# Two hybrid backbone layers on one core: where the residual is scaled, and in which order the up-projection's operands are made

## The chip, the cores and the metric

One core of one Trainium2 chip runs the whole program. The metric is the device time of one execution in microseconds (us), taken as the median of several runs.

The engines are named as in the profile. PE is TensorE, and PEld is its weight load. DVE is VectorE, ACT is ScalarE and POOL is GpSimd. SP is the engine from whose queue most transfers are issued. Some transfers are issued from POOL's queue; here these are the ones that add to what lies at the destination (`accum_op=ALU.add`).

## What is computed

The reference runs two layers over 1024 latent tokens and 256 context tokens, 1024 channels wide. Each layer mixes tokens (attention, a gated recurrence, a Fourier mix, one output projection) and then runs a gated feed-forward network with a width-3 convolution. What matters here is the end of each sub-layer:

```python
x1 = layer_norm(ALPHA * x + g1 * mix, ln1_g[l], ln1_b[l])
ffn = conv_ffn(x1 * (1 + sc2) + sh2, w_up[l], conv_w[l], conv_b[l], w_down[l])
x = layer_norm(ALPHA * x1 + g2 * ffn, ln2_g[l], ln2_b[l])

def conv_ffn(h, w_up, conv_w, conv_b, w_down):
    u = h @ w_up
    up = jnp.pad(u, ((0, 0), (1, 1), (0, 0)))
    u = up[:, :-2] * conv_w[0] + up[:, 1:-1] * conv_w[1] + up[:, 2:] * conv_w[2] + conv_b
    a, g = jnp.split(u, 2, axis=-1)
    return (a * jax.nn.silu(g)) @ w_down
```

So `ALPHA * x1`, the residual of the second update, is the normalised row times `ALPHA * ln1_g` plus `ALPHA * ln1_b`. All values are fp32. Layer 0 treats both streams, layer 1 only the latent one.

## The kernel before

**Matmuls.** A product of two fp32 operands is made from three passes: each operand is split into a high part, rounded by ACT, and a low part, the difference, made by DVE or POOL (`mm3`, lines 156 to 161). A "split" below is that pair of instructions.

**Order on the engines.** The program is written as one stream. A scheduler then places the instructions of each engine, by its own estimate of when each becomes ready, so the order on an engine need not be the order of the text. Each engine and each issuing queue then works strictly in its own order. Tiles of one tag share `bufs` buffers; a new tile waits until the readers of the old one are done.

**Output projection** (`out_tile`, line 1037). Ten tiles of 128 tokens in layer 0, eight in layer 1, in stages that overlap. A tile loads its residual (`resid_in`), multiplies with `w_out` (16 accumulations of three matmuls), adds and normalises (`normalise`), stores the normalised row to `y1[i]` (line 1071) and then stores its transpose to `yT` (`put_T`). In layer 1 the residual is multiplied by a row `ga` on POOL (line 1009), and a row `ba`, prepared by a load, a multiply on ACT and a store (lines 1700 to 1704), is added by an accumulating transfer (line 1010). While the last tiles run, `later_half` (line 1165) makes the operands B11 and B21 from the later 512 tokens, its low parts on POOL.

**Up-projection.** The 2816 pairs of columns are 22 blocks `j`. For each block the four quarter-products of a 2x2 scheme are made from seven smaller ones, listed in `ORDER` (line 1202): a weight operand (A11, A12, A22 or a sum S1 to S4) times a data operand (B11, B21, B22 or a combination T1 to T4), each 12 matmuls of 512 columns. For the first six blocks (`EARLY`) the two products with B11 and B21 need only the later tokens. `up_early` (line 1192) makes them ahead and parks them in DRAM, two blocks inside the output projection's stage and four after it.

`combined_halves` (line 1171) makes the other five data operands. It goes through the four quarters `k` of the channels: it loads and modulates the four raw pieces of a quarter, makes T1 to T4 of that quarter, and splits all five operands of that quarter; T1 and T4 get their low parts on POOL. It is called between the last four `up_early`.

`up_all` (line 1239) then goes through blocks 0 to 21. A block writes into two tiles U of 128x1026 (value and gate). For an early block the parked product comes back by a transfer into U's later half (lines 1269 and 1289); the first product is added to it, and the third accumulates onto the first one's PSUM bank. `gate(j)` runs the convolution on each half of both tiles (two DVE instructions each, line 1120), the gating, and one store per half. `up_weights` sums and splits each weight operand by itself, 128x512 at a time (lines 1219 and 1231 to 1233).

**Down-projection** (`down_all`, line 1403). The same scheme: seven products P1, P7, P6, P4, P5, P3, P2 in that order, each in six steps over 11 blocks. Weight and activation operands are put together in place by accumulating transfers from POOL's queue (`plus`, line 1344). The residual of a tile comes in `load_r`, which `PLAN` (line 1466) ties to a product and a step: the four later tiles in P6 steps 2 to 5, the four earlier ones where `DOWN_AT` says.

```python
nc.scalar.copy(r[:, 0:1], after)                # load_resid, lines 992 to 999: after = a value of this step
nc.sync.dma_start(out=r, in_=src)
e0.tensor_tensor(out=r, in0=r, in1=ga, op=ALU.mult)   # DVE in down_all, POOL in ffn_down
e1.tensor_tensor(out=r, in0=r, in1=ba, op=ALU.add)
```

In layer 0 the context tokens' feed-forward follows (`ffn_up`, `ffn_down`, line 1511); there the two instructions on `r` stand on POOL, two tiles.

Of the kernel before, what the change touches and what calls it, by code (L numbers as in the profile page):

```python
# [19 lines left out]
P = 128  # L20
D = 1024
# [34 lines left out]
DOWN_AT = ((("P34", "P35", "P23", "P24"), ("P21", "P22", "P24", "P25"), ("P21", "P22", "P24", "P25"), ("P21", "P22", "P23", "P24")),  # L56
           (("P34", "P35", "P21", "P22"), ("P21", "P22", "P23", "P24"), ("P21", "P22", "P23", "P24"), ("P34", "P35", "P20", "P21")))
# [39 lines left out]
def hybrid_backbone_kernel(ctx: ExitStack, tc: tile.TileContext, A: dict, out: bass.AP):  # L97
# [890 lines left out]
    def load_resid(pp, src, ga, ba, bufs=4, after=None, engs=None):  # L988
        r = pp.tile([P, D], F32, tag="r", bufs=bufs, name="r")
        if after is not None:  # L990

            nc.scalar.copy(r[:, 0:1], after)
        nc.sync.dma_start(out=r, in_=src)
        if ga is None:
            nc.scalar.mul(r, r, ALPHA)
        else:
            e0, e1 = engs or (nc.gpsimd, nc.gpsimd)
            e0.tensor_tensor(out=r, in0=r, in1=ga, op=ALU.mult)
            e1.tensor_tensor(out=r, in0=r, in1=ba, op=ALU.add)
        return r  # L1000

    def resid_in(src, late):
        pp, _, ga, ba = late
# [33 lines left out]
    def out_tile(l, i, S, pa, late, wo, src, y1, yT):  # L1037
# [22 lines left out]
        pp, g1 = late[0:2]  # L1060
# [86 lines left out]
    def h_pair(hp, nm):  # L1147
        return tuple(hp.tile([P, 4, HALF], F32R, name=nm + x) for x in "hl")

    def load_quarter(rp, yT, t0, k, cols, tag, bufs, eng=None):  # L1150
        r = rp.tile([P, HALF], F32, tag=tag, bufs=bufs, name="hraw")
        nc.sync.dma_start(out=r, in_=yT[k * P:(k + 1) * P, CTX + t0:CTX + t0 + HALF])
        a, b = (c[:, k:k + 1] for c in cols)
# [6 lines left out]
    def split_to(pair, k, src, eng):  # L1160
        hi, lo = (t[:, k, :] for t in pair)
# [9 lines left out]
    def combined_halves(h, rp, yT, cols):  # L1171
        for k in range(4):
            b11, b21, b12, b22 = (load_quarter(rp, yT, t0, kk, cols, f"raw{t0}{kk // 4}", 1 if t0 else 2, e)
                                  for t0, kk, e in ((HALF, k, nc.scalar), (HALF, k + 4, nc.scalar), (0, k, None), (0, k + 4, None)))
            yield
            t1, t2, t3, t4 = (rp.tile([P, HALF], F32, tag=f"t{x}", bufs=1, name="hcomb") for x in range(4))
            for o, x, y in ((t1, b12, b11), (t2, b22, t1), (t3, b22, b12), (t4, t2, b21)):
                nc.vector.tensor_tensor(out=o, in0=x, in1=y, op=ALU.subtract)
            yield
            for nm, src, eng in (("T2", t2, nc.vector), ("T1", t1, nc.gpsimd), ("T3", t3, nc.vector), ("T4", t4, nc.gpsimd),  # L1180
                                 ("B22", b22, nc.vector)):
                split_to(h[nm], k, src, eng)
            yield

    def up_product(w, b, bank, onto=None):
        acc = psu([P, HALF], "pu", bank) if onto is None else onto
        for k in range(4):
            mm3(acc, tuple(t[:, k, :] for t in w), tuple(t[:, k, :] for t in b), k == 0 and onto is None, k == 3,
# [13 lines left out]
    ORDER = (("A11", "B11"), ("A12", "B21"), ("S2", "T2"), ("S1", "T1"), ("S3", "T3"), ("A22", "T4"), ("S4", "B22"))  # L1202

    def up_weights(l, fp):
# [8 lines left out]
        def operand(j, nm):  # L1213
            if nm[0] == "A":
                return quarter(j, nm)
            if (j, nm) not in made:
                for o, x, y, op in (("S1", "A21", "A22", ALU.add), ("S2", "S1", "A11", ALU.subtract),
                                    ("S3", "A11", "A21", ALU.subtract), ("S4", "A12", "S2", ALU.subtract)):
                    t = fp.tile([P, 4, P], F32, tag=o, bufs=1, name=o)
# [4 lines left out]
        def splits(todo):  # L1224
            for n, (j, nm) in enumerate(todo):
                if n % 2 == 0:
                    own = n // 2 % 5 > 2
# [635 lines left out]
```

## Time and profile before

| | us |
|---|---|
| median of 3 runs | 3336.25 (3333.35 to 3342.41) |
| the profiled execution's own time | 3349.57 |
| its span in the profile | 3347.8 |
| PE busy, share of the span | 3098.0 (93%) |
| DVE busy | 2363.9 (71%) |
| ACT busy | 1585.6 (47%) |
| POOL busy | 772.6 (23%) |

The profiled execution is 13.3 us longer than the median. A busy PE is not PE at its peak: the granted clock (PEclk, 1.00 is 2.4 GHz, 0.50 is 1.2 GHz) says at what rate it ran. In the span, layer 0's output projection ends and `up_early` runs until 926.8; its up-projection runs from 946.3 to about 1395, its down-projection to 1640, the context tokens' part to about 1860. Layer 1's up-projection runs from 2665.7 to about 3083, its down-projection to 3322.

### The profile page before, as it was taken

The page shows a single profiled execution, that of the slowest core. Times are in us where ns is not written, and L with a number is a line of the kernel's source. Part 1 is how long each engine was busy: PE and PEld are TensorE (multiplying, and loading weights), DVE is VectorE, ACT ScalarE, POOL GpSimd, SP SyncE. Part 2 cuts the span into 40 slices and gives each one's busy share as a digit, 9 for nine tenths or more (in the row PEclk, how much of TensorE's full clock was granted, in tenths as well). Part 3 has the DMA queues.
Part 4 walks back from the last instruction along what each step waited for, and adds up shares of the span by engine and source line. Part 5 has one row for each costly group of instructions (what it writes and reads, how often), then busy time and mean ns, then how long its engine had stood idle before and what let it go on. Part 6 is the DMA issues. An engine that isn't in the chain of part 4 may idle for free.

```text
span 3347.8 us, 55191 instructions
## 1 busy us (share of the span) xinstructions
PE 3098.0 (93%) x20897; PEld 2526.6 (75%) x20897; DVE 2363.9 (71%) x4377; ACT 1585.6 (47%) x3169; POOL 772.6 (23%) x820
## 2 busy tenths in 40 slices
PE   6999998999979999999999999998978789999996
PEld 4878977787756777677797788876767677887785
DVE  4623567887687877668876754668777778887678
ACT  3324556674444544434454435655652434554332
POOL 3522114432210000021245351115425300000222
PEclk9999999999989999999999999998889899999998
DMA  7652232107655444597775432122028632223973
GB/s 216 201 159 80 59 98 58 39 15 237 212 186 158 129 130 131 162 252 197 235 211 173 133 106 71 47 85 73 21 82 228 207 110 85 85 76 116 277 185 126
DMA packets 450255, 456.51 MB, mean 136 GB/s; under 512 B 31859, under 2 KB 343620, under 8 KB 449990
## 3 DMA queue, kind: packets, MB, share of 16 engines
q1 hardware_dynamic: 420006, 404.53, 38.4%
q0 software_dynamic: 29984, 48.46, 7.7%
q8 instruction: 164, 2.69, 0.3%
q14 instruction: 101, 0.83, 0.1%
HBM read 358.36 MB, written 94.55 MB: 135 GB/s over the span
## 4 chain that ended last, share of the span: by engine, by line
PE 47%; DVE 11%; DMA 5%; POOL 3%; issue 2%; ACT 2%; SPq 1%; POOLq 0%; DVEq 0%; ACTq 0%
PE pu L159 9%; PE pu L160 8%; PE pu L161 8%; PE pd L159 3%; PE pd L160 3%; PE pd L161 3%; PE ps_t L603 2%; PE ps_s L567 1%; PE ps_o L613 1%; DMA araw<-act 1%; DVE cv L1120 1%; DVE wlo L1387 1%; PE ps_s L568 1%; PE pws L159 1%; PE ps_o L615 1%
## 5 line engine op out<-in xcount | busy, mean ns | idle before, releaser
L570 DVE TENSOR_REDUCE mx<-ps_s 128x1 f32<-128x512 f32 (+1 forms) x400 | 222.4, 588 | 109.7 <-PE ps_s L568 108.6
L1345 POOL DMA_DIRECT2D X<-in_w_down_dram x48 | 55.4, 1154 | 1028.9 <-DMA X<-in_w_down_dram 945.1
L609 DVE TENSOR_TENSOR pl<-ps_t,ph 128x512 fp32r<-128x512 f32 x328 | 223.0, 686 | 88.1 <-ACT ph L608 86.1
L603 PE MATMUL ps_t<-ident,p 128*128 128x128 f32 x1312 | 265.5, 286 | 14.2 <-DVE pl L609 8.7
L608 ACT CAST ph<-ps_t 128x512 fp32r<-128x512 f32 x328 | 191.0, 589 | 162.8 <-PE ps_o L615 81.7
L577 ACT ACTIVATE p<-ps_s,mx 128x512 f32<-128x512 f32 (+1 forms) x400 | 243.2, 617 | 52.2 <-DVE mx L573 42.4
L160 PE MATMUL pd<-wlo,whi 128*128 128x512 f32 x616 | 248.4, 403 | 14.0 <-DVE wlo L1387 12.3
L159 PE MATMUL pd<-whi,wlo 128*128 128x512 f32 x616 | 242.8, 401 | 16.9 <-DVE wlo L1387 12.7
L1120 DVE SCALAR_TENSOR_TENSOR cv<-U,cw,cv 128x512 f32<-128x512 f32 x352 | 247.1, 748 | 12.9 <-ACT cv L1117 12.8
L161 PE MATMUL pd<-whi 128*128 128x512 f32 x616 | 247.7, 402 | 0.0
L159 PE MATMUL pxs<-whi,hlo 128*128 128x256 f32 x752 | 221.5, 295 | 5.8 <-DVE hraw L1566 4.3
L145 POOL TENSOR_TENSOR wlo<-raw,whi 128x1024 fp32r<-128x1024 f32 x63 | 152.5, 2423 | 281.0 <-ACT whi L144 281.0
L160 PE MATMUL pxs<-wlo,hhi 128*128 128x256 f32 x752 | 216.5, 288 | 0.6 <-DVE wlo L145 0.4
L161 PE MATMUL pxs<-whi,hhi 128*128 128x256 f32 x752 | 216.2, 288 | 0.0
L613 PE MATMUL ps_o<-pl,V 128*128 128x256 f32 x656 | 202.8, 326 | 6.6 <-DVE pl L609 4.0
L603 PEld LDWEIGHTS ps_t<-ident,p 128*128 128x128 f32 x1312 | 166.2, 144 | 38.2 <-DVE pl L609 14.7
L1117 ACT ACTIVATE cv<-U,cb,cw 128x512 f32<-128x512 f32 x176 | 138.1, 815 | 111.4 <-DVE U L1248 99.3
L615 PE MATMUL ps_o<-ph,V 128*128 128x256 f32 x656 | 184.7, 299 | 0.0
L1232 ACT CAST whi<-S 128x512 fp32r<-128x512 f32 x176 | 106.4, 620 | 149.2 <-PE pu L161 113.3
L144 ACT CAST whi<-raw 128x1024 fp32r<-128x1024 f32 x130 | 136.0, 1049 | 84.3 <-DMA raw<-in_w_up_dram 30.7
L567 PE MATMUL ps_s<-KT,qt 128*128 128x512 f32 (+1 forms) x400 | 150.8, 408 | 6.4 <-ACT p L577 3.0
L159 PEld LDWEIGHTS pxs<-whi,hlo 128*128 128x128 f32 x752 | 143.5, 191 | 15.3 <-issue 7.4
(401 smaller groups left out, 9160.4 us busy)
## 6 DMA issues: line engine op xcount, KB each, us to landing
raw<-in_w_up_dram SPq DMA_DIRECT2D x144, 512.0 KB
raw<-in_w_ada_dram SPq DMA_DIRECT2D x96, 512.0 KB
raw<-in_w_down_dram SPq DMA_DIRECT2D x52, 512.0 KB
act<-cv SPq DMA_DIRECT2D x88, 256.0 KB
X<-in_w_down_dram POOLq DMA_DIRECT2D x40, 512.0 KB, 9.6
raw<-in_w_in_dram SPq DMA_DIRECT2D x36, 512.0 KB
y<-r SPq DMA_DIRECT2D x28, 512.0 KB
araw<-act SPq DMA_DIRECT2D x26, 512.0 KB
```

What stands on the lines that cost most here:

```text
L159: nc.tensor.matmul(o, lhsT=al, rhs=bh, start=start, stop=False, skip_group_check=onto)
L160: nc.tensor.matmul(o, lhsT=ah, rhs=bl, start=False, stop=False, skip_group_check=onto)
L161: nc.tensor.matmul(o, lhsT=ah, rhs=bh, start=False, stop=stop, skip_group_check=onto)
L567: nc.tensor.matmul(t[:, 0:n], lhsT=qt[:, h % (2 * QT_PAIRS), :], rhs=KT[:, 2 * kv + 1, s0:s0 + n], start=True, stop=False)
L570: nc.vector.tensor_reduce(out=mx[:, j:j + 1], in_=t[:, 0:n], axis=AX.X, op=ALU.max)
L577: nc.scalar.activation(out=t, in_=sc[j][:, 0:n], func=AF.Exp, bias=mx[:, 3:4], accum_out=su[:, h, j:j + 1])
L603: nc.tensor.transpose(t[:, ss, h, :], in_=ps2[h][2 * s2 + ss], identity=ident)
L608: nc.scalar.copy(ph, tv)
L609: nc.vector.tensor_tensor(out=pl, in0=tv, in1=f32(ph), op=ALU.subtract)
L613: nc.tensor.matmul(o, lhsT=V[:, s, kv, 1:3, :].rearrange("p a c -> p (a c)"), rhs=pl[:, ss, :], start=(s == 0), stop=False)
L615: nc.tensor.matmul(o, lhsT=V[:, s, kv, 0:2, :].rearrange("p a c -> p (a c)"), rhs=ph[:, ss, :], start=False, stop=(s == nk - 1))
L1120: nc.vector.scalar_tensor_tensor(out=o, in0=u[:, tap:tap + n], scalar=convw[l][tap][:, c:c + 1], in1=o, op0=ALU.mult, op1=ALU.add)
```

## The change

1. `out_tile` stores `y1` later: after `put_T` the row is multiplied by a new row `gn` = `ALPHA * ln1_g` on POOL, then stored. A new DRAM row `bn` = `ALPHA * ln1_b` is made by `scaled_row` (load, ACT multiply, store).
2. `load_resid` fills `r` with `bn`, broadcast by a transfer from SP, and adds `y1` by an accumulating transfer from POOL. The two multiplying and adding instructions are gone, as are the loads of the rows `ga` and `ba` in `rows`. The tag `r` has 8 buffers instead of 6; the earlier tiles' loads are in P5, steps 2 to 5.
3. `combined_halves` goes operand by operand: all B11 and B21 pieces, then T2 for all quarters, then T1, T3, B22, T4. All low parts are on DVE. Its tiles reuse each other's places.
4. Six weight operands are split ahead (`ready_w`) between the steps of 3. Blocks 6 and 7 go first, then 0 to 5, then the rest. In `ORDER` S4 comes before A22. Two operands that lie side by side are split by one pair of 128x1024 instructions.
5. `gate` works on 1024 columns at once, value first, and stores once.

```diff
-DOWN_AT = ((("P34", "P35", "P23", "P24"), ("P21", "P22", "P24", "P25"), ...
-           (("P34", "P35", "P21", "P22"), ("P21", "P22", "P23", "P24"), ...
+DOWN_AT = ((("P52", "P53", "P54", "P55"), ("P21", "P22", "P24", "P25"), ...
+           (("P52", "P53", "P54", "P55"), ("P21", "P22", "P23", "P24"), ...
...
+    def load_resid(pp, src, b, after):
+        r = pp.tile([P, D], F32, tag="r", bufs=8, name="r")
+        nc.scalar.copy(r[:, 0:1], after)
+        nc.sync.dma_start(out=r, in_=b.partition_broadcast(P))
+        nc.gpsimd.dma_start(out=r, in_=src, accum_op=ALU.add)
         return r
 
+    def scaled_row(pp, src, nm):
+        t = pp.tile([KD, P], F32, tag="brow", bufs=1, name="brow")
+        nc.sync.dma_start(out=t, in_=src.rearrange("(k p) -> k p", p=P))
+        nc.scalar.mul(t, t, ALPHA)
+        o = scratch(nm, [D])
+        nc.sync.dma_start(out=o.rearrange("(k p) -> k p", p=P), in_=t)
+        return o
...
         normalise(pp, r)
-        nc.sync.dma_start(out=y1[i], in_=r)
         tag = yield
         put_T(r, yT, i * P, pp, tag=tag or "u")
+        nc.gpsimd.tensor_tensor(out=r, in0=r, in1=gn, op=ALU.mult)
+        nc.sync.dma_start(out=y1[i], in_=r)
...
+        for k in range(4):
+            b11.append(fetch("B11", place("T3h", k), k, nc.scalar))
+            b21.append(fetch("B21", place("B22l", k), k, nc.scalar))
             yield
+        for k in range(4):
+            b12.append(fetch("B12", place("B22h", k), k, nc.scalar))
+            b22.append(fetch("B22", place("raw2", k), k))
+            t1.append(sub(place("T3l", k), b12[k], b11[k]))
+            t2.append(sub(place("raw1", k), b22[k], t1[k]))
+            split_into("T2", k, t2[k])
             yield
+        for k in range(4):
+            split_into("T1", k, t1[k])
+            yield
+        for k in range(4):
+            split_into("T3", k, sub(place("T4h", k), b22[k], b12[k]))
+            yield
+        t4 = [sub(t2[k], t2[k], b21[k]) for k in range(4)]
+        for k in range(4):
+            split_into("B22", k, b22[k])
+            yield
+        for k in range(4):
+            split_into("T4", k, t4[k])
             yield
...
-    ORDER = (..., ("S3", "T3"), ("A22", "T4"), ("S4", "B22"))
+    ORDER = (..., ("S3", "T3"), ("S4", "B22"), ("A22", "T4"))
...
+                if nm == "A22":
+                    hl, n = [fp.tile([P, 512], F32R, tag=t + "y", bufs=2, name=t) for t in ("whi", "wlo")], 4
+                    src = operand(j, nm)
+                else:
+                    todo.pop(0)
+                    own = wide % 4 == 3
+                    wide += 1
+                    hl = [(fp if own else wp).tile([P, 1024], F32R, tag=t + "x" * own, bufs=1 if own else 3, name=t)
+                          for t in ("whi", "wlo")]
+                    n = KD
...
-        todo = [(j,) + o for j in range(NJ) for o in ORDER if ...]
+        todo = [(j,) + o for j in chain(range(EARLY, EARLY + 2), range(EARLY), range(EARLY + 2, NJ)) for o in ORDER if ...]
...
+            cv = []
+            for part in (0, 1):
+                o = fp.tile([P, SEQ], F32, tag=f"cv{part}", bufs=1, name=f"cv{part}")
+                conv(l, j, part, o, U[part])
+                if part:
+                    nc.scalar.activation(out=o, in_=o, func=AF.Silu)
+                cv.append(o)
             for t0 in (HALF, 0):
...
-                nc.sync.dma_start(out=act[j, :, t0:t0 + HALF], in_=cv[1])
+            nc.sync.dma_start(out=act[j, :, :], in_=cv[0])
...
+            gn = bcast_row(pp, A["ln1_g"][l, :], "gn", "gn", ALPHA)
+            bn = scaled_row(pp, A["ln1_b"][l, :], f"bn{l}")
...
             for j in range(2, EARLY):
                 up_early(l, j, h2, ep, "early", parked)
-                for _ in range(3):
+                for _ in range(2):
+                    next(prep, None)
+
+            ready_w = []
+            for n in (4, 2):
+                ready_w += [next(uw) for _ in range(n)]
+                for _ in range(4):
                     next(prep, None)
```

## Rows read from the trace of the kernel before

**Rows 1.** what PE waited for in the whole span: engine, line, releaser; us, times, longest us.
```profile
PE pu L159 <- ACT whi L1232: 39.4, 2, 19.9
```

**Rows 2.** stretches: PE, PEld, DVE, ACT, POOL busy us (instructions); granted clock, DMA share, GB/s.
```profile
926.80:946.30 19.50, 0.01 (x1) 0.04 (x1) 19.50 (x31) 11.51 (x19) 9.87 (x6) 0.60 0.51 165
...
946.30:951.10 4.80, 4.80 (x11) 3.76 (x12) 4.80 (x9) 1.91 (x4) 0.00 (x0) 0.50 0.39 112
...
946.30:1075.00 128.70, 121.91 (x575) 87.19 (x576) 102.24 (x169) 45.92 (x73) 0.00 (x0) 0.95 0.55 170
...
2665.70:2784.00 118.30, 103.95 (x411) 81.63 (x412) 94.81 (x151) 43.07 (x70) 0.00 (x0) 0.93 0.37 109
...
2830.00:3060.00 230.00, 230.00 (x994) 184.68 (x993) 191.46 (x300) 119.42 (x196) 0.00 (x0) 1.00 0.25 79
...
1406.00:1550.00 144.00, 138.58 (x568) 110.41 (x569) 97.35 (x104) 55.64 (x65) 39.77 (x35) 0.94 1.06 257
...
1550.00:1582.00 32.00, 31.62 (x137) 25.14 (x136) 25.52 (x49) 16.02 (x26) 1.89 (x4) 1.00 0.38 127
...
3272.00:3312.00 40.00, 33.52 (x126) 25.23 (x125) 39.23 (x46) 12.68 (x16) 7.12 (x6) 0.91 0.53 184
...
1810.00:1840.00 30.00, 25.15 (x97) 18.81 (x96) 19.10 (x12) 11.43 (x18) 20.15 (x8) 0.94 0.41 143
...
2525.00:2605.00 80.00, 74.01 (x342) 59.76 (x343) 61.21 (x120) 24.73 (x44) 42.30 (x44) 0.96 0.76 211
```

**Rows 3.** timeline of DVE in layer 0's preparation of operands: start us, us, line.
```profile
915.47 1.00 DVE L1157 TENSOR_SCALAR hraw<-hraw,ma,mb 128x512 f32<-128x512 f32 x2
...
941.75 0.68 DVE L1163 TENSOR_TENSOR T2l<-hcomb,T2h 128x512 fp32r<-128x512 f32 x1
...
942.35 0.68 DVE L1163 TENSOR_TENSOR T3l<-hcomb,T3h 128x512 fp32r<-128x512 f32 x1
```

**Rows 4.** timeline of SP and DVE around one early block of layer 1.
```profile
2708.32 0.38 SPq L1269 DMA_DIRECT2D U<-up  x1
...
2713.88 0.69 DVE L1248 TENSOR_TENSOR U<-pu,U 128x512 f32<-128x512 f32 x1 [1.96 <-DMA U<-up]
...
2717.69 0.69 DVE L1248 TENSOR_TENSOR U<-pu,U 128x512 f32<-128x512 f32 x1 [1.80 <-PE pu L161]
...
2728.57 0.32 SPq L1269 DMA_DIRECT2D U<-up  x1
...
2731.42 0.69 DVE L1248 TENSOR_TENSOR U<-pu,U 128x512 f32<-128x512 f32 x1
```

**Rows 5.** line 998, the residual's multiply: durations ns min/median/max.
```profile
L998 DVE TENSOR_TENSOR r<-r,ga x16: 1167/1222/1227, 1486.3 to 3303.5; 128x1024 f32<-128x1024 f32 x16
```

**Rows 6.** line 999 on POOL in the context tokens' part: durations ns min/median/max.
```profile
L999 POOL TENSOR_TENSOR r<-r,ba x2: 2467/2860/3252, 1809.4 to 1824.7; 128x1024 f32<-128x1024 f32 x2
```

**Rows 7.** timeline of POOL and DVE in layer 1's output projection.
```profile
2572.72 2.39 POOL L1009 TENSOR_TENSOR r<-r,ga 128x1024 f32<-128x1024 f32 x1
...
2572.90 3.03 DVE L1054 TENSOR_TENSOR ml<-mr,mh 128x768 fp32r<-128x768 f32 x1
```

**Rows 8.** timeline of SP in the same stage, its start.
```profile
2491.30 0.33 SPq L1701 DMA_DIRECT2D brow<-in_ln_b_dram  x1
...
2502.43 0.32 SPq L1704 DMA_DIRECT2D ba<-brow  x1
```

**Rows 9.** DMA queues in 1440 to 1570: packets, MB, share of 16 engines.
```profile
q0 software_dynamic: 7495, 14.37, 62.2%
...
q1 hardware_dynamic: 7480, 15.21, 34.4%
```

**Rows 10.** timeline of POOL and DVE in layer 0's down-projection.
```profile
1416.17 1.19 POOL L1345 DMA_DIRECT2D X<-in_w_down_dram  x1 [9.37 <-DMA X<-in_w_down_dram]
...
1531.90 1.18 POOL L1345 DMA_DIRECT2D X<-in_w_down_dram  x1 [2.91 <-DVE wlo L1387]
...
1553.29 1.22 DVE L1387 TENSOR_TENSOR wlo<-X,whi 128x1024 fp32r<-128x1024 f32 x1
```

More of the change, by code (lines that the diff above doesn't have):

```diff
@@ L986, in post_half @@
         nc.vector.tensor_tensor(out=r[:, sl], in0=r[:, sl], in1=tmp, op=ALU.add)
[L988 to L999, printed above, removed]
-        return r
+    def load_resid(pp, src, b, after):
[3 more added lines that the diff above has]
+        nc.gpsimd.dma_start(out=r, in_=src, accum_op=ALU.add)
+        return r
+    def scaled_row(pp, src, nm):
[5 more added lines that the diff above has]
+        return o
     def resid_in(src, late):
-        pp, _, ga, ba = late
+        pp, _, ga, ba, _ = late
         r = pp.tile([P, D], F32, tag="r", bufs=4, name="r")
@@ L1147, in h_pair @@
     def h_pair(hp, nm):
-        return tuple(hp.tile([P, 4, HALF], F32R, name=nm + x) for x in "hl")
+        return tuple([t[:, k, :] for k in range(4)] for t in (hp.tile([P, 4, HALF], F32R, name=nm + x) for x in "hl"))
     def load_quarter(rp, yT, t0, k, cols, tag, bufs, eng=None):
@@ L1169, in later_half, with combined_halves, place, fetch @@
             yield
-    def combined_halves(h, rp, yT, cols):
+    def combined_halves(h, hp, rp, yT, cols):
+        def place(nm, k, dt=F32):
+            return (rp if nm[0:3] == "raw" else hp).tile([P, HALF], dt, tag=f"{nm}{k}", bufs=1, name=nm)
+        def fetch(nm, r, k, eng=None):
+            kk, t0 = k + 4 * (nm[1] == "2"), HALF if nm[2] == "1" else 0
+            nc.sync.dma_start(out=r, in_=yT[kk * P:(kk + 1) * P, CTX + t0:CTX + t0 + HALF])
+            return modulated(r, kk, cols, eng)
+        def sub(o, x, y):
+            nc.vector.tensor_tensor(out=o, in0=x, in1=y, op=ALU.subtract)
+            return o
+        def split_into(nm, k, src):
+            hi, lo = (place(nm + x, k, F32R) for x in "hl")
+            nc.scalar.copy(hi, src)
+            nc.vector.tensor_tensor(out=lo, in0=src, in1=f32(hi), op=ALU.subtract)
+            for t, x in zip(h[nm], (hi, lo)):
+                t.append(x)
+        for nm in ("T2", "T1", "T3", "T4", "B22"):
+            h[nm] = ([], [])
+        b11, b21, b12, b22, t1, t2 = ([] for _ in range(6))
@@ L1200, in up_early @@
             nc.sync.dma_start(out=parked[j, x], in_=t)
-    ORDER = (("A11", "B11"), ("A12", "B21"), ("S2", "T2"), ("S1", "T1"), ("S3", "T3"), ("A22", "T4"), ("S4", "B22"))
+    ORDER = (("A11", "B11"), ("A12", "B21"), ("S2", "T2"), ("S1", "T1"), ("S3", "T3"), ("S4", "B22"), ("A22", "T4"))
     def up_weights(l, fp):
@@ L1218, in operand @@
                                     ("S3", "A11", "A21", ALU.subtract), ("S4", "A12", "S2", ALU.subtract)):
[L1219 removed]
+                    pair = "S21" if o in ("S1", "S2") else "S34"
+                    if (j, pair) not in made:
+                        made[j, pair] = fp.tile([P, KD, P], F32, tag=pair, bufs=1, name="S")
+                    h = 4 * pair[1:].index(o[1])
+                    t = made[j, pair][:, h:h + 4, :]
                     nc.vector.tensor_tensor(out=t, in0=operand(j, x), in1=operand(j, y), op=op)
@@ L1722, in hybrid_backbone_kernel @@
         hp = h2s.enter_context(pool(f"h2c{l}", side=side_b))
-        h2.update({nm: h_pair(hp, nm) for nm in ("T1", "T2", "T3", "T4", "B22")[::-1 if side_b == "right" else 1]})
         ups = ExitStack()
```

86 lines of the change are left out of this document (33 added, 53 removed).

## The prediction

> **What bounds the kernel now.** I read PE's waits first, because PE is busy most of the span, and then asked by stretches where it is not. One line of the waits stands out: the up-projection's first pass waited twice, 39.4 us together [rows 1]. The stretches put the first wait at 926.8 to 946.3: PE does nothing, while DVE is busy in all of its 19.5 us [rows 2]. So at this place DVE sets the time, not PE. DVE's timeline says with what: the operands of all four quarters, begun at 915.5, the last at 942.4 [rows 3]; no product can be finished before that, since each needs four quarters. Layer 1 repeats this. After the gap the granted clock is 0.50, the 1.2 GHz level, and 11 matmuls take 4.80 us [rows 2]. In full blocks 994 matmuls take 230 us at 1.00, 0.2314 us each, with PE never idle while DVE is busy for 191 us [rows 2]: there PE alone is the bound.
>
> The six early blocks lie between. From 2665.7 to 2784 PE ran 411 matmuls, worth 95.1 us, in 118.3 us; 2.3 of the missing 23.2 us are the restart. The timeline shows the ring behind it [rows 4]: U is free and the parked product's transfer goes out at 2708.3, is added at 2713.9, the third product is added at 2717.7, and the next transfer goes out at 2728.6. That is 20.3 us a block, and an early block holds PE only for 60 x 0.2314 = 13.9 us.
>
> **The operands, quarter by quarter against one by one.** Today's loss is 19.7 us of idle time and 4.8 - 2.5 = 2.3 us at the lower clock, 22.0 a layer. For the new one I price a 512-wide DVE instruction at its spacing, 0.60 us [rows 3], and a 1024-wide one at 1.2 [rows 5]. T2 of all quarters is 16 instructions (b12's modulation moves to ACT), 9.6 us; T1, T3, B22 and T4 are 24 more, 14.4 us. POOL's eight splits are in this. Between them DVE must do block 6's four sums and A22's split (3.0), three wide splits (3.6), three adds of the early products (1.8) and four evacuations (2.4), 10.8 in all. From 915.5 T2 is ready after 9.6 and some 6 us of the rest, at 931.1; the last quarter of T4 at 950.3. PE comes free at 926.8, but block 6 now stands first and its products with B11 and B21 take 24 matmuls, 5.6 us: T2 is asked for at 932.4, T4 at 943.5, and its product would end at 946.3. It ends at 951.0, so about 4.7 us are lost. Gain 17 a layer, **34 in all**. At best nothing is lost (22 a layer); at worst the last quarter of T2 is left behind the rest and PE waits 950.3 - 932.4 = 17.9 us plus the restart, a gain of 2. I take 17 because DVE already works at this spacing without a gap.
>
> **The early blocks.** The ring in the new order: transfer and add 2.9 to 5.6 us (the two in rows 4), mean 4.2; third product and add 3.8; reissue and reload 0.7 + 4.2; then one 1024-wide ACT instruction (no row; taken as DVE's 1.2) and two DVE instructions, 2.4, after which the value tile is free, because `gate` takes value first and S4 comes before A22. That is 16.5 against 20.3. Five old rings should have cost 5 x (20.3 - 13.9) = 32 us and cost 20.9, so 11 were covered by PE running ahead. Six new ones cost 6 x 2.6 - 11 = 4.6: a gain of 16; with the slow transfer twice, 19.3 a ring, nothing; with the fast one 21. I take **13**. In layer 0 the conditioning matmuls fill: 6.8 us idle and 5% of 128.7 at the lower clock, less the restart, leave 10.9 [rows 2]; I take **5** (0 to 9). Running blocks 6 and 7 first removes no work. It moves the queue: six parked reloads now stand behind two full blocks' weights on SP, which wait for PE anyway.
>
> **Wide splits, wide gate, one store.** They save DVE and ACT time in full blocks, where PE is busy 230 of 230 us and DVE 191 [rows 2]. **Nothing** gained; PE hides it. Were that cover gone, a block would cost DVE's 16 us, still under PE's 19.4.
>
> **The residual in the down-projection.** Sixteen multiplies and adds leave DVE in each layer, 1.2 us each [rows 5]. They count only where DVE is the last to finish: from 3272 to 3312 DVE is busy 39.2 of 40 us, and PE loses 6.5 us idle and 9% of 40 to the clock, 10.1 [rows 2]. Eight stand there, 9.4 us. I take **7** (0 to 10), and nothing in layer 0. In the context tokens' part POOL loses two pairs of 2.4 + 2.9 us [rows 6] and gets two issues of 1.2; it waited for the rows' landing before too. PE lost 4.9 us idle and 1.8 to the clock there [rows 2]; I take **4** (0 to 6.7).
>
> What comes in is DMA work. In 1440 to 1570 accumulating transfers took 0.622 x 130 = 80.9 us of the engines for 14.37 MB, plain ones 44.7 for 15.21 [rows 9]: 2.95 and 1.54 us for 512 KB. The broadcast replaces the load of y1, so a layer gains 8 x 2.95 less the two rows no longer loaded, 20.5 us. Four of the eight fall into a stretch with DMA share 1.06, +8.7 us; P5's fall where the share is 0.38, 20 of 32 us free [rows 2]. The operands have room: the last accumulation is issued at 1531.9, lands some 9 us later and is split at 1553.3 [rows 10], so 12 us to spare. **Nothing** (0 to 18 lost for both layers).
>
> **The residual where it is made.** Eighteen multiplies of 2.39 us [rows 7] enter POOL's queue, each behind its tile's transposes and ahead of the next tile's small steps; y1's store waits, which the down-projection doesn't notice. POOL was busy 42.3 of 80 us in layer 1's stage, and PE lost 6.0 us there [rows 2]. With five more multiplies POOL has 54. I take **6 lost** (0 to 20, half of all 43). The row bn adds a load, a multiply and a store to SP's queue: the like chain took from 2491.3 to 2502.4 [rows 8], and behind it stand the tiles' loads. I take **2 lost** (0 to 11).
>
> **Sum.** 34 + 13 + 5 + 7 + 4 - 6 - 2 = 55 us. The profiled execution's own 3349.57 becomes 3294.6. It stands 13.3 above the median, a difference the change has no part in; the median becomes 3336.25 - 55 = **3281**. All best ends give 91 (3245), all worst ones -45 (3381).
>
> **Rivals.**
> (1) The wait moves. DVE, POOL's splits now on it, is late for T3 and T4, and the parked transfers keep their slow end: 10 a layer at the gap, 3 at the early blocks, 7 and 4 as above, 8 lost. 26 us, **3310**. For it: DVE has 34.8 us of work in a stretch of 35.5. Against: its instructions get shorter without POOL beside them. Chance 0.18.
> (2) The written order isn't the order run, since the scheduler places each engine's work itself. The gap stays (2 a layer), the rings give 3, the down-projection 4 and 4, 8 lost: 7 us, **3329**, no change. Against: even today operands and weights interleave by readiness. 0.08.
> (3) Slower: POOL's queue in P6. Each accumulation of y1 must wait for its broadcast to land, and in the full stage POOL once waited 9.37 us for such a load [rows 10]. Four in front of the accumulations that P5 needs are 37.5 us; beyond the 12 to spare, PE waits 25.5 a layer, with a restart 27.8, and the 8.7 of DMA come on top: 73 us for both. 3281 + 73 = **3354**, 18 slower. It decides once POOL issues those more than 12 us later than now. Against: the four come one a step, and a step is 24 matmuls, 5.6 us, so the queue catches up. 0.07.
> (4) POOL's multiplies hold DVE. Beside the 2.39 us multiply a 128x768 subtraction on DVE took 3.03 us [rows 7], longer than the 1.2 of a 1024-wide one. If every new multiply held DVE for all of it on PE's path, 43 us are lost in place of 6: **3318**. Against: PE has other tiles' matmuls then. 0.06.
> The Trainium skill, page "SBUF — State Buffer", section "SBUF: two separate sides", says that GpSimd and a VectorE instruction with two SBUF inputs exclude each other for a whole instruction. By that rule the sum is rival 4's; the row agrees that DVE waits, not that PE does.
>
> **Numbers.** The forecast has 0.61. Faster by over 0.3% (10 us, about what can be told from no change) are forecast, (1) and (4): 0.85; same (2): 0.08; slower (3): 0.07. The range leaves out (2) and (3) and runs from 3252, most best ends together, to 3322, which holds (1) and (4).
>
> **What would show it.** Right: the wait on `whi` gone from PE's list, the first T2 product some 6 us after the last early one; T3 products of early blocks about 17 us apart; no DVE stretch of 40 full us near the end. Wrong: PE idle over 10 us after the early products with DVE full; the new accumulation on POOL waiting over 5 us a time with P5's matmuls late; out-projection stretches longer by more than 10 us a layer.

## The result: 30 us slower, where 55 faster were forecast

| | us |
|---|---|
| changed kernel, median of 6 runs | 3370.55 (3356.70 to 3375.58) |
| kernel before, median of 6 runs | 3340.86 (3333.35 to 3347.96) |
| ratio | 1.0083, 95% interval 1.0066 to 1.0101 |
| profiled execution of the changed kernel, its span | 3359.95, 3358.1 |

By the medians the changed kernel is 29.7 us slower; the ratio's interval makes that 22 to 34. The two traces differ by only 10.3 us of span: the execution profiled before was a long one, the one after a short one. A third of the missing 19.4 us lies in layer 1's attention, which the change doesn't touch (6.6 us; there the granted clock from 2200 to 2400 is 0.94 after and 0.91 before). The other 13 aren't located.

To see where the time went, I cut both traces where the same products are done: at the first and the last one of each output projection, at the last one of each up-projection (B22's in the kernel before, T4's in the changed one, since `ORDER` changed) and at the last one of each down-projection. Each column is the time between two such starts; the last one ends with the span. Here and below a row of such a table is one profiled execution, so a few us of a single figure can be chance.

| kernel | before it | out-proj 0 | up 0 | down 0 | context | attention 1 | out-proj 1 | up 1 | down 1 | tail |
|---|---|---|---|---|---|---|---|---|---|---|
| before | 763.0 | 127.9 | 508.4 | 237.9 | 214.0 | 639.9 | 119.9 | 473.5 | 241.0 | 22.3 |
| changed | 763.2 | 139.6 | 500.3 | 249.9 | 202.8 | 633.3 | 131.2 | 470.6 | 252.0 | 15.2 |
| difference | 0.2 | 11.7 | -8.1 | 12.0 | -11.2 | -6.6 | 11.3 | -2.9 | 11.0 | -7.1 |

Both output projections and both down-projections got longer, and the up-projections, where 52 us were forecast, gave 11.

PE's waits (us, times, longest), first two lines of the kernel before, beside [rows 1]:

```profile
PE pd L159 <- DVE wlo L1387: 12.7, 7, 5.9
...
PE pwo L159 <- DVE ml L970: 6.9, 3, 3.0
```

and in the changed kernel:

```profile
PE pd L159 <- DVE wlo L1447: 28.0, 12, 6.5
PE pwo L159 <- DVE ml L970: 24.8, 7, 7.6
PE pu L159 <- DVE wlo L1291: 22.0, 2, 11.9
...
PE pwo L159 <- DVE ml L1057: 13.6, 3, 6.1
...
PE pu L160 <- DVE T4l L1195: 7.3, 2, 3.7
```

The 39.4 us on `whi` are gone, but 22.0 on a weight's low part and 7.3 on T4's stand in the same two places. The first two lines have grown, from 12.7 and 6.9: operands of the down-projection, and the mixed rows of the output projection.

Stretches of the changed kernel, with the columns of [rows 2]:

```profile
915.00:930.00 15.00, 15.00 (x70) 12.21 (x69) 7.26 (x9) 5.85 (x8) 2.41 (x1) 1.00 0.92 303
...
938.90:972.20 33.30, 18.52 (x59) 13.77 (x58) 32.25 (x55) 18.21 (x29) 0.00 (x0) 0.74 0.46 137
2655.60:2689.70 34.10, 16.78 (x56) 12.95 (x56) 33.00 (x55) 18.70 (x31) 0.00 (x0) 0.75 0.34 101
...
2705.00:2833.80 128.80, 116.16 (x481) 91.16 (x480) 103.85 (x128) 45.54 (x47) 0.00 (x0) 0.97 0.36 111
...
1406.00:1578.00 172.00, 160.56 (x665) 127.39 (x665) 106.70 (x123) 60.95 (x78) 47.20 (x43) 0.96 1.07 263
1578.00:1600.00 22.00, 15.51 (x48) 11.89 (x47) 19.00 (x35) 12.24 (x19) 1.90 (x4) 0.75 0.32 111
...
2525.00:2605.00 80.00, 65.32 (x287) 53.20 (x286) 60.54 (x110) 21.26 (x36) 49.48 (x46) 0.88 0.72 195
```

**The gap moved.** In 938.9 to 972.2, from the last early product to the end of T2's first, PE ran 59 matmuls, 13.7 us at 0.2314, in 33.3: 19.6 lost. In layer 1 it is 34.1 - 56 x 0.2314 = 21.1. Before it was 22.0 each. The first line shows what is missing: from 915 to 930, where [rows 3] show DVE already making operands, DVE is busy for 7.26 of 15 us.

**The early blocks** of layer 1 (2705.0 to 2833.8) lost 128.8 - 481 x 0.2314 = 17.5 us, against 20.9.

**The down-projection.** The stretch with all DMA engines busy (share 1.07) now lasts until 1578; before it ended at 1550 [rows 2]. Behind it PE works for only 15.5 of 22 us, at 0.75 of the clock.

**The output projection** of layer 1: PE 65.3 of 80 us, where it was 74.0 [rows 2]; POOL 49.5, where it was 42.3.

POOL and DVE there, at one of PE's longest waits (7.1 us, until 2598.17):

```profile
2557.91 2.67 POOL L1076 TENSOR_TENSOR r<-r,gn 128x1024 f32<-128x1024 f32 x1
...
2590.06 1.60 POOL L1170 TENSOR_TENSOR B11l<-hraw,B11h 128x512 fp32r<-128x512 f32 x1
2591.36 2.59 POOL L1076 TENSOR_TENSOR r<-r,gn 128x1024 f32<-128x1024 f32 x1
2593.66 1.51 POOL L1170 TENSOR_TENSOR B11l<-hraw,B11h 128x512 fp32r<-128x512 f32 x1
...
2557.40 3.74 DVE L986 TENSOR_TENSOR r<-r,tmp 128x512 f32<-128x512 f32 x1
...
2590.77 5.22 DVE L1057 TENSOR_TENSOR ml<-mr,mh 128x768 fp32r<-128x768 f32 x1
...
2597.72 0.40 DVE L970 TENSOR_TENSOR ml<-pr,mh 128x256 fp32r<-128x256 f32 x1
```

POOL has three instructions without a pause, the new multiply in the middle, from 2590.06 to 2595.17. DVE's subtraction begins in the first of them and ends after the last: 5.22 us. Behind it in DVE's queue stands the small L970, for which PE waits. PE's longest wait for it (7.6 us, until 2562.72) has the same neighbours: the addition of line 986, 0.69 us as a rule, took 3.74 beside the new multiply.

The operands of layer 0: SP's queue (start, us it was at it), then DVE:

```profile
923.67 0.41 SPq L1185 DMA_DIRECT2D T3h<-yT  x1
...
930.72 0.45 SPq L1185 DMA_DIRECT2D B22l<-yT  x1
933.82 0.32 SPq L1243 DMA_DIRECT2D up<-early  x1
934.18 0.92 SPq L1185 DMA_DIRECT2D B22h<-yT  x2
...
937.92 0.69 DVE L1189 TENSOR_TENSOR T3l<-B22h,T3h 128x512 f32<-128x512 f32 x1 [3.40 <-ACT B22h L1162]
```

All pieces of B11 (place T3h) and B21 (B22l) go ahead of B12's, between stores of parked products that wait for PE; the first B12 (B22h) is asked for at 934.18. So DVE makes its first combination at 937.92, where the forecast had it start at 915.5.

PE where T4's product stands, in the order run:

```profile
961.16 0.49 PE L159 MATMUL pu<-T4h,wlo 128*128 128x512 f32 x1 [1.02 <-ACT T4h L1194]
965.33 0.79 PE L160 MATMUL pu<-T4l,whi 128*128 128x512 f32 x1 [3.67 <-DVE T4l L1195]
...
967.63 0.63 PE L159 MATMUL pu<-T2h,wlo 128*128 128x512 f32 x1
```

After block 6's first product, which waited for the low part of its weight until 949.2, the order is B21, T1, T4, T2. T4's product stands ahead of T2's, though its operand is made last: the scheduler put it there.

One early block of layer 1 on DVE and SP, against [rows 4]:

```profile
2767.31 1.42 DVE L1307 TENSOR_TENSOR U<-pu,U 128x512 f32<-128x512 f32 x2 [2.56 <-PE pu L161]
2768.77 0.69 DVE L1307 TENSOR_TENSOR U<-U,pu 128x512 f32<-128x512 f32 x1
2770.83 1.28 DVE L1124 SCALAR_TENSOR_TENSOR cv<-U,cw,cv 128x1024 f32<-128x1024 f32 x1 [1.37 <-ACT cv L1121]
2772.11 0.69 DVE L1307 TENSOR_TENSOR U<-pu,U 128x512 f32<-128x512 f32 x1
2772.72 1.28 DVE L1124 SCALAR_TENSOR_TENSOR cv<-U,cw,cv 128x1024 f32<-128x1024 f32 x1
2773.91 1.22 DVE L1291 TENSOR_TENSOR wlo<-S,whi 128x1024 fp32r<-128x1024 f32 x1
2775.05 1.28 DVE L1124 SCALAR_TENSOR_TENSOR cv<-U,cw,cv 128x1024 f32<-128x1024 f32 x1
2776.25 0.68 DVE L1268 TENSOR_TENSOR S<-raw 128x512 f32<-128x512 f32 x1
2776.85 1.28 DVE L1124 SCALAR_TENSOR_TENSOR cv<-U,cw,cv 128x1024 f32<-128x1024 f32 x1
...
2778.19 0.32 SPq L1329 DMA_DIRECT2D U<-up  x1
...
2781.89 0.69 DVE L1307 TENSOR_TENSOR U<-pu,U 128x512 f32<-128x512 f32 x1 [0.23 <-DMA U<-up]
```

The first convolution on DVE starts at 2770.83, before the last addition to U at 2772.11: the tile that is ready first goes first, whatever the text says. The parked product is asked for again at 2778.19, when the fourth convolution instruction ends; between the four stand a split and a sum of the weights. T3 products of these blocks are 17.8 to 19.4 us apart, 18.4 in this one.

### The profile page after: what moved, and what is told of

Same layout as the page of the kernel before. It is cut to its first block, busy times and chain, and to the rows that moved or that the text cites. A ratio compares the mean times of both kernels' runs of the same rounds, so it can differ in the third digit from the quotient of the medians.

```text
span 3358.1 us, 54451 instructions
## 1 busy us (share of the span) xinstructions
PE 3103.7 (92%) x20897; PEld 2526.6 (75%) x20897; DVE 2306.8 (69%) x4057; ACT 1540.8 (46%) x2925; POOL 788.5 (23%) x836
## 4 chain that ended last, share of the span: by engine, by line
PE 45%; DVE 12%; DMA 11%; POOL 4%; issue 4%; ACT 2%; SPq 0%; POOLq 0%; DVEq 0%; ACTq 0%
PE pu L159 9%; PE pu L160 9%; PE pu L161 9%; DMA araw<-act 3%; PE ps_t L603 2%; PE pd L159 1%; DMA r<-y 1%; PE pd L161 1%; PE pd L160 1%; PE ps_s L567 1%; PE ps_o L613 1%; DVE wlo L1447 1%; PE ps_s L568 1%; PE ps_o L615 1%; DMA raw<-in_w_up_dram 1%
## 5 line engine op out<-in xcount | busy, mean ns | idle before, releaser
L1124 DVE SCALAR_TENSOR_TENSOR cv<-U,cw,cv 128x1024 f32<-128x1024 f32 x176 | 223.9, 1281 | 36.0 <-ACT cv L1121 35.4
L159 PEld LDWEIGHTS pd<-whi,wlo 128*128 128x128 f32 x616 | 119.6, 195 | 74.4 <-DVE wlo L1447 27.8
L1121 ACT ACTIVATE cv<-U,cb,cw 128x1024 f32<-128x1024 f32 x88 | 109.4, 1244 | 111.2 <-DVE U L1307 110.5
L159 PE MATMUL pwo<-whi,ml 128*128 128x512 f32 x288 | 121.7, 424 | 39.0 <-DVE ml L970 24.8
```

The costliest lines, as they stand in the source:

```text
L159: nc.tensor.matmul(o, lhsT=al, rhs=bh, start=start, stop=False, skip_group_check=onto)
L1124: nc.vector.scalar_tensor_tensor(out=o, in0=u[:, tap:tap + n], scalar=convw[l][tap][:, c:c + 1], in1=o, op0=ALU.mult, op1=ALU.add)
```

## The experiments

Ratios are to the kernel before, run on the same chip. A difference to the changed kernel, or between two experiments, is one of medians, in part from different chips; the kernel before had medians from 3341 to 3343 beside all of them. Stage times, cut as above:

| kernel | median | out-proj 0 | up 0 | down 0 | context | out-proj 1 | up 1 | down 1 | tail |
|---|---|---|---|---|---|---|---|---|---|
| e1 residual part alone | 3384.61 | 140.5 | 507.0 | 256.9 | 205.1 | 128.6 | 480.0 | 251.7 | 15.0 |
| e2 up-projection part alone | 3325.36 | 130.4 | 500.9 | 235.4 | 212.7 | 120.4 | 467.0 | 241.2 | 21.9 |
| e3 multiply on DVE | 3348.55 | 133.0 | 500.3 | 252.9 | 201.0 | 121.8 | 473.1 | 251.0 | 14.7 |
| e4 plain transfer, no bn | 3329.66 | 140.2 | 503.8 | 235.2 | 201.1 | 132.6 | 471.4 | 235.6 | 15.8 |
| e6 two transfers in P5 only | 3353.66 | 139.0 | 505.9 | 243.6 | 203.2 | 131.4 | 472.6 | 243.2 | 15.1 |
| e7 two transfers in P6 only | 3345.43 | 138.7 | 502.3 | 242.5 | 202.6 | 132.1 | 472.1 | 242.1 | 15.2 |
| e8 plain, from POOL's queue | 3334.20 | 138.5 | 501.9 | 234.4 | 201.3 | 132.5 | 471.8 | 236.4 | 15.0 |
| e9 adding, no broadcast | 3344.70 | 139.7 | 505.0 | 241.9 | 202.8 | 131.7 | 471.9 | 241.6 | 14.9 |
| e10 broadcast, no adding | 3351.60 | 139.8 | 500.8 | 245.2 | 203.1 | 132.3 | 471.5 | 246.3 | 14.6 |
| e11 other fetch order | 3312.54 | 129.9 | 492.8 | 234.0 | 214.2 | 120.8 | 460.4 | 243.5 | 21.9 |
| e12 and T4 earlier | 3318.65 | 132.0 | 493.4 | 233.9 | 214.9 | 118.5 | 461.4 | 245.4 | 21.9 |
| e13 bytes without POOL | 3350.44 | 140.3 | 500.7 | 246.6 | 203.2 | 132.7 | 471.5 | 238.9 | 15.8 |
| e14 POOL's wait without bytes | 3334.13 | 139.3 | 505.0 | 233.6 | 202.6 | 129.7 | 471.2 | 238.1 | 15.8 |
| e15 put together | 3327.44 | 131.2 | 494.6 | 241.7 | 210.3 | 126.7 | 462.9 | 242.4 | 16.4 |

### The two halves

e1 is the kernel before with points 1 and 2 of the change, e2 with points 3 to 5:

```diff
 e1: load_resid, scaled_row, out_tile's multiply and later store, DOWN_AT, rows()   as changed
 e2: combined_halves, up_weights, ORDER, todo, gate, ready_w                       as changed
```

> The kernel before with the residual part alone (rows scaled in the output projection, bn by two transfers, eight buffers, loads in P5); the up-projection stays as before. Theory A (the loss is in the residual part: output projection +11 us a layer, down-projection +9 in layer 0, about +1 in layer 1 with the tail, -11 in the context part): 15 to 30 us slower than before. Theory B (the loss comes from the new up-projection order, which also shifts everything behind it): within 5 us of before.

> The kernel before with the up-projection part alone (operand order, blocks 6 and 7 first, wide splits, wide gate); the residual stays as before. Theory A (the gap only moved: 21 us of 22 are still lost in each layer, the early blocks give back 0 to 5): 0 to 6 us faster than before. Theory B: 15 to 30 slower. The prediction's own terms for this part would have given 52 faster.

Measured: e1 1.0137 (1.0118 to 1.0157), 43 us slower; e2 0.9959 (0.9944 to 0.9973), 16 faster. Together 27 slower, about what the whole change costs (30). Theory B falls. Theory A holds in its sign and had both sizes too small. e2's gain lies in its up-projections, 7.5 and 6.5 us shorter than before. Counted as above, its gaps lose 16.9 and 15.3 us, against 19.6 and 21.1 in the whole change: the residual part delays the operands too.

### POOL's multiply

```diff
-        nc.gpsimd.tensor_tensor(out=r, in0=r, in1=gn, op=ALU.mult)
+        nc.vector.tensor_tensor(out=r, in0=r, in1=gn, op=ALU.mult)
```

> The changed kernel with the row's multiply by gn on DVE instead of POOL. Theory A1 (POOL's multiply holds DVE in the middle of PE's path): DVE's own multiply is 1.2 us, the 5 us subtractions beside it go back to about 1 to 3, and the output projection gets shorter by 5 to 10 us a layer, 10 to 20 in all against the changed kernel. Theory A2 (the row's later store or the order is what costs, not the engine): within 4 us of the changed kernel, or slower, as DVE gains 22 us of work.

Measured: 1.0030 (1.0011 to 1.0048), 22 us under the changed kernel's median; the output projections fall by 6.6 and 9.4 us. The 18 subtractions of line 1057 (durations in ns, least, median, most), first in the changed kernel, where three are stretched (1.95, 2.50 and 5.22 us):

```profile
L1057 DVE TENSOR_TENSOR ml<-mr,mh x18: 900/948/5224, 762.1 to 2590.8; 128x768 fp32r<-128x768 f32 x18
```

and with the multiply on DVE:

```profile
L1057 DVE TENSOR_TENSOR ml<-mr,mh x18: 903/951/960, 763.8 to 2584.9; 128x768 fp32r<-128x768 f32 x18
```

None is stretched any more. Theory A1 holds: 16 of the 23 us of the two output projections come from the multiply standing on POOL, beside DVE. In neither kernel does PE wait there for a result of POOL for more than 0.4 us. The work that DVE gained, 25.5 us (median 1.21 a multiply, 3.21 at most), is mostly hidden.

### The two transfers

```diff
 e4:
-        nc.sync.dma_start(out=r, in_=b.partition_broadcast(P))
-        nc.gpsimd.dma_start(out=r, in_=src, accum_op=ALU.add)
+        nc.sync.dma_start(out=r, in_=src)
```

> The changed kernel with the residual tile of the down-projection filled by one plain transfer from SP; the row bn is left out of the sum, so neither the broadcast nor the accumulating transfer is there. Theory C1 (the added transfers and POOL's wait for them lengthen the down-projection): layer 0's down-projection falls from 250 us to 241 or less, layer 1's from 252 to 244 or less, 15 to 25 us faster than the changed kernel. Theory C2 (the down-projection is longer because of the later loads, not of what they move): within 5 us of the changed kernel.

Measured: 0.9968 (0.9953 to 0.9983), 41 us under the changed kernel, more than C1 had; the down-projections are 14.7 and 16.4 us shorter. C1 holds. The stretch with full DMA engines ends about as early as before:

```profile
1406.00:1552.00 146.00, 138.42 (x568) 109.64 (x569) 94.68 (x101) 55.81 (x68) 40.20 (x35) 0.95 1.06 259
1552.00:1600.00 48.00, 47.51 (x202) 37.50 (x201) 42.54 (x75) 24.03 (x36) 4.26 (x8) 1.00 0.50 172
```

Some of the same work lies behind that stretch, so I took the DMA engines' busy time (the mean of the 16) over the whole stage, from the last product of the up-projection to the last one of the down-projection: 229.8 and 212.8 us in the two layers of the changed kernel, 210.2 and 191.7 in e4, 210.3 and 191.8 in the kernel before. The two transfers cost the engines 19.6 and 21.1 us more, for eight tiles.

Then the place (e6, e7: the plain transfer for one half of the tiles) and the parts (e8 to e10):

```diff
 e6/e7:  def load_resid(pp, src, b, after, two=True)     two = i < NCT + 4 / i >= NCT + 4
 e8:   - broadcast, adding transfer     + nc.gpsimd.dma_start(out=r, in_=src)
 e9:   - broadcast                      + nc.vector.memset(r, 0.0)
 e10:  - accum_op=ALU.add
```

> The changed kernel where only the four earlier tiles' residuals (loaded in P5) are put together by two transfers; the four later ones (P6) come by one plain transfer, bn left out of them. Theory C1a (it is the transfers in P6's stretch, where the DMA engines are already full, that cost): the down-projections fall to 235 to 240 us. Theory C1b (each accumulating transfer costs its share wherever it is): about half the loss stays, 242 to 245 us.

> The changed kernel where only the four later tiles' residuals (loaded in P6) are put together by two transfers; the four earlier ones (P5) come by one plain transfer, bn left out of them. Theory C1a: the down-projections stay at 247 to 252 us. Theory C1b: about half the loss goes, 242 to 245 us.

> The changed kernel with the residual tile filled by one plain transfer issued from POOL's queue, where the accumulating one stood; bn is left out of the sum. POOL's queue then has the same issues, but none waits for a broadcast to land, and the engines move half as much. Theory Q (POOL's queue standing behind the broadcasts, up to 19 us a time, is what delays the operands), and theory V (the volume of the added transfers is) both give 235 to 238 us for the down-projections here; over 242 us would mean that it is the issues themselves in POOL's order.

> The changed kernel where DVE fills the residual tile with zeros instead of the broadcast of bn (bn is left out of the sum); the accumulating transfer from POOL stays. POOL then waits for no transfer before it issues it. Theory Q (POOL's queue standing behind the broadcasts is the cost): down-projections 235 to 240 us, as without bn. Theory V (what the accumulating transfers move and how long it takes): 245 to 252 us.

> The changed kernel with both transfers of the residual tile, but the one from POOL overwrites instead of adding (bn is lost from the sum). POOL's queue waits for each broadcast as in the changed kernel; the second transfer is a plain one. Theory Q: 245 to 252 us in the down-projections. Theory V: 236 to 242 us.

Measured: e6 1.0026 (1.0013 to 1.0040), e7 1.0008 (0.9994 to 1.0022), e8 0.9980 (0.9965 to 0.9995), e9 1.0005 (0.9990 to 1.0020), e10 1.0031 (1.0015 to 1.0046). Either half of the tiles costs about half (6.5 to 8.4 us a layer over e4): C1b. An issue in POOL's queue costs nothing (e8). By medians over e4 the adding costs 15 us (e9) and the broadcast 22 (e10), together close to the 41. Neither Q nor V alone gave these two numbers, and in e9 POOL still waited for the fill, which is new work on DVE as well. So two more runs:

```diff
 e13:  t = pp.tile([P, D], F32, tag="bnd", bufs=1, name="bnd")
       nc.sync.dma_start(out=t, in_=b.partition_broadcast(P));  nc.sync.dma_start(out=r, in_=src)
 e14:  nc.sync.dma_start(out=r, in_=src)
       nc.gpsimd.tensor_scalar(out=r[:, 0:1], in0=r[:, 0:1], scalar1=1.0, scalar2=None, op0=ALU.mult)
```

> The changed kernel with the residual tile filled by one plain transfer from SP, and beside it the broadcast of bn into a tile that nobody reads (ring of seven for room; bn is left out of the sum). The engines move as many bytes for a tile as with two transfers, none of them accumulating, and POOL's queue has no part in it. Theory V (volume): 243 to 248 us in the down-projections, as in the run with broadcast and no add. Theory Q (POOL's queue waiting): 234 to 238.

> The changed kernel with one plain transfer from SP, and one tiny multiply by 1.0 on POOL (one column) that has to wait until the tile has landed, where the accumulating transfer stood; bn is left out of the sum. POOL's queue then stands behind a landing as in the changed kernel, but nothing more is moved than with the plain transfer. Theory Q: 243 to 248 us in the down-projections. Theory V: 234 to 238.

Measured: e13 1.0021 (1.0006 to 1.0036), e14 0.9979 (0.9963 to 0.9995). POOL's wait for the residual tile in layer 0's down-projection, first in the changed kernel:

```profile
POOL r L994 <- DMA r<-bn: 26.9, 4, 19.1
```

and in e14:

```profile
POOL r L994 <- DMA r<-y: 30.8, 7, 15.2
```

POOL's queue stood as long in e14 as in the changed kernel, and the kernel is within 5 us of e4's. With the bytes and without POOL it is 21 us slower than e4, as e10 is. So theory Q falls, and by the medians theory V holds. In layer 1 the profiled e13 shows only 3.3 us of it, and 11.4 in layer 0; that execution (span 3338.3) was the shortest of its eight runs.

The traces show a second thing, which neither theory has. DVE adds to the residual tiles loaded in P5 (line 1485), and in its queue low parts of weights stand behind these additions. In the changed kernel, with PE's wait last:

```profile
1563.17 0.69 DVE L1485 TENSOR_TENSOR r<-r,p 128x512 f32<-128x512 f32 x1 [5.47 <-DMA r<-y]
...
1574.77 0.69 DVE L1485 TENSOR_TENSOR r<-r,p 128x512 f32<-128x512 f32 x1 [3.38 <-DMA r<-y]
1575.38 0.68 DVE L1447 TENSOR_TENSOR wlo<-Y,whi 128x512 fp32r<-128x512 f32 x1
...
1576.12 0.80 PE L159 MATMUL pd<-whi,wlo 128*128 128x512 f32 x1 [5.20 <-DVE wlo L1447]
```

By run, in us, layer 0 and layer 1:

| kernel | DMA engines' time over e4 | DVE waiting for r's transfer | down-projection over e4 |
|---|---|---|---|
| e4 plain | 0, 0 | 0, 1.0 | 0, 0 |
| e13 bytes without POOL | 11.5, 10.6 | 0, 0 | 11.3, 3.3 |
| e7 two transfers in P6 only | 9.6, 10.6 | 0, 1.4 | 7.3, 6.5 |
| e6 two transfers in P5 only | 10.5, 9.9 | 7.6, 11.7 | 8.4, 7.6 |
| changed | 19.6, 21.1 | 9.6, 14.5 | 14.7, 16.4 |

In P6 the engines' time is left as the cost: DVE doesn't wait for r there (e7), and POOL's queue is out (e14). In P5 (e6) that time and DVE's wait for the landing come together, and no run takes them apart. e13 doesn't either: in layer 0 its broadcasts are all issued by 1513, well before P5's loads at 1549.

### The operands' order

```diff
 e11, on e2:
-            b11.append(fetch("B11", ...)); b21.append(fetch("B21", ...))            # for all k, then b12, b22
+            b11.append(fetch("B11", ...)); b12.append(fetch("B12", ...)); yield; b22.append(fetch("B22", ...)); ...
+            b21.append(fetch("B21", ...)); split_into("T1", k, t1[k])              # for all k, after T2
 e12, on e11:   T4 split ahead of T3 and B22 (T3's source in B12's place)
```

> The kernel with the up-projection part alone, with the raw pieces fetched in another order: B11, B12 and B22 of a quarter together, and the four B21, which only T4 needs, after them. Theory F (the new order lets DVE stand idle until 928 us, because the first combination waits behind eight other fetches in SP's queue): DVE starts its combinations 5 to 10 us earlier, the up-projection stages fall by 5 to 10 us each, 10 to 20 us faster than the up-projection part alone (3325). Rival G (T4's product stands third on PE, and its low part is made last, so PE waits for the end of DVE's list whenever that begins): under 4 us a layer.

> As the run before, and T4 is split before T3 and B22, since PE takes T4's product third. Theory G: the wait for T4's low part goes, 5 to 8 us a layer less than with the fetch order alone. Theory F alone: no further change, within 3 us of the run before; T3 or B22 becomes the wait.

Measured: e11 0.9900 (0.9877 to 0.9924), 13 us under e2 and 29 under the kernel before; e12 0.9927 (0.9906 to 0.9947). e11's stretches:

```profile
915.00:930.00 15.00, 15.00 (x66) 12.08 (x65) 13.98 (x23) 12.81 (x21) 0.00 (x0) 1.00 0.86 284
...
925.00:948.90 23.90, 14.91 (x57) 11.08 (x55) 23.59 (x41) 14.63 (x24) 0.00 (x0) 0.79 0.60 185
```

DVE is busy for 13.98 of the 15 us, where it was 7.26 in the changed kernel and 7.27 in e2, and the gap's loss is 23.9 - 57 x 0.2314 = 10.7, against 16.9 in e2. Theory F holds. With T4 made earlier (e12) PE's wait moves to ACT's copy of the first product (3.8 us) and nothing is won: rival G falls.

### Versions with the whole residual

e5 makes the whole row on DVE and loads it by one plain transfer; e15 is the changed kernel with e11's order, the multiply on DVE, and bn added by DVE in the down-projection:

```diff
 e5:   + nc.vector.tensor_tensor(out=r, in0=r, in1=gn, op=ALU.mult);  nc.vector.tensor_tensor(out=r, in0=r, in1=bnr, op=ALU.add)
 e15:  + nc.vector...(gn) in out_tile;  load_resid: nc.sync.dma_start(out=r, in_=src);  eng.tensor_tensor(out=r, in0=r, in1=b, op=ALU.add)
```

> The changed kernel with the finished row (times gn, plus bn) made by two DVE instructions in the output projection and loaded in the down-projection by one plain transfer; three residual buffers instead of four in the output projection, to make room for the row bn. It computes what the reference does. Theory A1+C1 (POOL's multiply and the added transfers are what the residual part costs): down-projections as without bn (235 and 236 us), output projections 133 to 137 and 122 to 126 us; 3310 to 3325 us, 16 to 30 faster than before. Rival (DVE is the bound in the output projection, or three buffers are too few): output projections over 140 and 132 us, 3335 or more.

> A version put together from the runs: the changed kernel with the other fetch order, the multiply by gn on DVE in the output projection, and bn added in the down-projection by one DVE instruction (POOL in the context part) to a tile that one plain transfer fills; ring of seven. It computes what the reference does. If the costs add up: output projections 133 and 122 us, up-projections 493 and 461, down-projections 236 to 240, context part 201 to 206; 3290 to 3308 us, faster than the kernel before and than the run with the fetch order alone (3312). Rival: the DVE instruction at the end of layer 1 gives back the tail, 3310 to 3320.

Measured: e5 0.9953 (0.9935 to 0.9971), 3327.49; the one execution that was profiled took 8694.99, far from its other six (3320.67 to 3333.06), so no stage is read from it. Its median lies between its two forecasts. e15 0.9952 (0.9933 to 0.9970): slower than its forecast (3290 to 3308) and than its rival's (3310 to 3320), and not for the rival's reason, since the tail stays short (16.4). Longer than its forecast are the down-projections (241.7 and 242.4), where DVE has the additions again and waits 12.9 and 11.8 us for r, the context part (210.3) and layer 1's output projection (126.7); what lengthens each wasn't tried. The best version stays e11, which leaves the residual as it was.

## Why the prediction was wrong

**The operands, 34 forecast: 3.3 measured** (22.0 - 19.6 and 22.0 - 21.1; in e2, without the residual part, 11.8). The step that failed is "From 915.5 T2 is ready after 9.6 and some 6 us of the rest". It gave DVE its list, and no fetch: the queue that the pieces come through was not gone through. Eight fetches of B11 and B21 stand ahead of the first B12, between stores that wait for PE, so the first combination came at 937.9 (928.8 in e2, whose output projection is shorter; 915.3 in e11). e11 shows the cost: with those fetches exchanged 8.1 and 6.6 us more come out of the two up-projections. The second failed step is "T2 is asked for at 932.4": block 6's third product on PE was T1's, its fourth T4's, and its first waited for a weight's low part behind the combinations on DVE. Rival (2) said that the order run need not be the one written; I gave it 0.08 for the whole kernel and should have asked for each product when its buffers are free.

**The early blocks, 13 and 5: 3.4 in layer 1, about 6 in layer 0** (the up-projection's 8.1 less the gap's 2.4, with whatever else changed there). Layer 0's term came out near its size; its ring wasn't looked at. In layer 1 the ring is 18.4 us in the block shown, not 16.5. The term for the 1024-wide ACT instruction and the two DVE instructions, 3.6, took 5.3: from the addition's end at 2772.80 to 2778.13. DVE puts a split and a sum between them, and the gate tile's convolution goes first.

**Wide splits, gate and store, nothing:** in layer 1 the gap and the early blocks (0.9 and 3.4) already make more than the up-projection's 2.9, so nothing is left for them, as forecast.

**The residual's work on DVE, 7: about 12.** From e2 to e4 layer 1's down-projection falls by 5.6 and the tail by 6.1; layer 0's by 0.2, as forecast. The tail was left out of the term. **The context part, 4: 11.6** (212.7 to 201.1). The mechanism was right, the size was not.

**The transfers, nothing (0 to 18 lost): 31 lost** (14.7 and 16.4 from e4). The size was right, 20.5 us of engine time a layer forecast and 19.5 and 21.0 measured over the kernel before. The cover failed. In P6, where 8.7 us a layer was the worst end, 7.3 and 6.5 were lost (e7). In P5 "20 of 32 us free" counted the engines' time and not who waits for the tile: there DVE waited 7.6 and 11.7 us for r ahead of the weights' low parts, and 8.4 and 7.6 us were lost (e6). Rival (3), POOL's queue, would have given the same sign by another cause; e8 and e14 exclude it.

**The multiply, 6 lost (0 to 20), with 2 for bn's chain: 23 lost.** The step "PE has other tiles' matmuls then", said against rival (4), failed: the stretched subtraction, or addition, stands on DVE ahead of the small subtraction that the next tile's products need. e3 shows 16 of the 23 to come from the multiply on POOL. The rest goes with DVE's own multiply, the later store and bn's chain, not separated.

All these terms as measured make about 18 us lost, as the two traces do outside the attention (17); the medians say 30, and the rest stays open.

The Trainium skill, page "SBUF — State Buffer", section "SBUF: two separate sides", which the prediction named and didn't go by, was right here: the 128x768 subtraction has two SBUF inputs and took 5.22 us beside POOL, 0.96 at most without its multiply.

The signs named for a wrong forecast came: over 10 us idle after the early products, output projections longer by over 10 us a layer, and P5's matmuls late, though behind DVE and not behind POOL's queue. The gains came to 36 us of the 63 forecast. Of the losses, the multiply with bn's chain stayed within its worst ends (23 of 31) and the transfers didn't (31 of 18). The range left out what decided, since the losing terms were bounded by single rows and not by what stands next to them.

## What to carry to other kernels

When operands are put in another order, go through the queue that fetches them and through the order that the scheduler really runs, not only through the engine that makes them; the earliest start is set by the last fetch of the first result. Free DMA time doesn't cover a transfer by itself: ask also which engine waits for its landing, and what stands behind that wait in the engine's order. Work moved from DVE to POOL isn't off DVE's path: here POOL's multiply stretched DVE's own instructions, 0.95 us to 5.22. And when two kernels are compared by stages, cut them where the same work is done: the last product of a stage need not be the same in both.

## What the runs showed of the hardware

DVE's subtraction didn't get its turn between POOL's instructions: its record covers three of them in a row (5.22 us, 2590.77 to 2595.99) and ends 0.82 us after the last, about the 0.95 that it takes by itself, while the longest one in the kernel before took 3.03 [rows 7]. And eight tiles, each put together by a broadcast and an adding transfer, cost the DMA engines 19.6 and 21.1 us more than by a plain one, 2.5 a tile. The estimate from [rows 9] was 2.95: 1.41 for adding (2.95 - 1.54) and 1.54 for the broadcast.
